# Splitting attention queries and keys where they are computed, and loading the gate weights first, in a hybrid decoder layer

## The chip, the cores and the metric

The kernel runs on one core of a Trainium2 chip. The metric is the device time of one execution in microseconds (us), the median of several. A core has a matrix engine (TensorE, PE in the profile; its weight loads are PEld), a vector engine (VectorE, DVE), an activation engine (ScalarE, ACT), a general engine (GpSimd, POOL) and a queue engine (SyncE, SP). Each runs its own instructions in program order and waits on semaphores for the others. Transfers between the device memory and the on-chip memory are DMAs, here issued by SP and by POOL, and carried out by 16 DMA engines that all queues share.

## The reference

One layer, 256 tokens, width 2048, all in fp32. `x` is normalised and multiplied by one wide projection; its columns feed two branches, which are gated, projected, merged and projected again.

```python
proj = rmsnorm(x, pre_norm_g) @ w_in
(a_q, a_k, a_v, a_g, a_lr, b_q, b_k, b_v, b_g, m_a, m_b) = split(proj)
# branch a: gated linear attention, 4 heads
gk  = log_sigmoid(a_lr @ gla_gk_w2 + gla_gk_b) / 16        # a_lr has 16 columns
o_a = rmsnorm(gla_chunked(a_q, a_k, a_v, gk), gla_norm_g) * silu(a_g)
# branch b: causal differential attention, 16 heads, two maps of width 64 each
p   = softmax(mask(q_m @ k_m.T / 8))                       # m = 0, 1
o_b = (p[0] - lam * p[1]) @ b_v
o_b = rmsnorm(o_b, diff_norm_g) * (1 - lam_init) * silu(b_g)
merged = sigmoid(m_a) * (o_a @ w_branch_a) + sigmoid(m_b) * (o_b @ w_branch_b)
out = x + rmsnorm(merged @ w_out, post_norm_g)
```

## The kernel before

**Products of parts.** Each fp32 operand is split into two parts, `hi` (a rounded copy, made by ACT) and `lo` (what is left, a DVE subtraction); a product is the sum of hi·hi, hi·lo and lo·hi. The weights come from one packed array: SP loads them as tiles `raw` of 1 MiB (128 x 2048) into three buffers, and each half of a tile is split by ACT (L263) and DVE (L264) some halves ahead of its use. A half is 8 matmuls with `hi` and 4 with `lo` (L452).

**Order of the work.** A recording layer takes the instructions as the code issues them and a scheduler orders each engine's program from a model of times; only those wrapped in `tc.keep_in_program_order` keep their place. The main line of the code is the stream of weight halves. Between halves, `pump()` advances generators ("tasks") by one turn each; a `yield` ends a turn.

1. First come the values of the linear-attention branch (`first_joint`, `token_major`), with the tasks `load_constants`, `forget_gate` and the sums of input columns.
2. The set stage computes more columns as six sets of block products with sums of weights, which POOL loads by adding DMAs (tiles `a`, `b`) and SP fills up (`c`). `others()` runs beside it and computes, among other columns, the attention queries `dq` and keys `dk` of head groups 0 and 1 (`EARLY`).
3. Then come the gates and scores of the linear attention, and after them the differential attention, group by group (`diff_heads(g)`, g = 0 to 3): the group's values `dv` and gates `ub`, for groups 2 and 3 its `dq` and `dk`, and one task `diff_pair(g, pair, values)` for each pair of heads, which runs while the columns of the next group or of the merge gates (`m02`, `m03`) and the first output products with `oah`/`oal` keep PE busy.
4. Last come the output products, the merge and the norm.

**Queries and keys.** A `dq` or `dk` tile holds a pair of heads (128 x 512 numbers, 256 KB). It is computed in fp32 by `head_part` and spilled to device memory whole by one POOL DMA (`spill`, L129). In turn 1 `diff_pair` fetches it back: `twice` (L946 to L950) writes it into both halves of the partitions, `dq` into the tile `kh` and `dk` into `kl`, four DMAs on SP. In turn 2 it makes the parts, in place: ACT rounds `kh` into `q2` (L964), DVE puts the rest into the other half of each map of `q2` (L967, twice), ACT rounds `kl` into `kh` (L968) and DVE subtracts (L969), so that `kh` and `kl` end up as the key's two parts. Then each head's scores are 8 matmuls with `kh` (L985) and `kl` (L986), DVE masks and takes maxima (L990, L991) and ACT exponentiates (L996, tiles `prob`).

**Gate weights.** `a_lr @ gla_gk_w2` needs the 16 x 1024 matrix `w2` in four copies, at partitions 0, 32, 64 and 96, in the tile `w2_raw` (`w_raw` in the trace). `load_constants` clears the tile with DVE (L336) and loads the copies with four POOL DMAs (L338) after its last mask tile. `forget_gate` takes the transposed `a_lr` (`lrt`), makes the parts of w2 (`w_s` on ACT L537, `w2h` on ACT L538, `w_s` on DVE L539) and multiplies them (L548, PE); ACT adds the bias into `gp` (L551) and goes on to the exponentials `e`. The tiles `r1h`, `s2h`, `s4h` and `r3h` that stand near it on ACT (L617) are parts of sums of the input.

Of the kernel before, what the change touches and what calls it, by code (L numbers as in the profile page):

```python
# [6 lines left out]
F32 = mybir.dt.float32  # L7
F32R = mybir.dt.float32r
BF16 = mybir.dt.bfloat16
U8 = mybir.dt.uint8  # L10
AF = mybir.ActivationFunctionType
ALU = mybir.AluOpType
AX = mybir.AxisListType

P = 128
D = 2048
S = 256
# [77 lines left out]
def hybrid_kernel(ctx: ExitStack, tc, xt, xn, preg, postg, w, w2, gkb, glag, lamv, diffg, ident_d, causal_d, lmask_d, out):  # L95
# [25 lines left out]

    def t2(shape, name):
        count[0] += 1
        return pools[0].tile(shape, F32, tag="t2", name=f"{name}_{count[0]}", bufs=5 if len(pools) == 1 else 12)

    def spill(t, name):
        count[0] += 1
        d = dram.tile(list(t.shape), t.dtype, name=f"{name}_{count[0]}")
        pool.dma_start(d, t)  # L129
        return d  # L130
# [10 lines left out]
    def f32(ap):  # L141
        return ap.bitcast(F32)
# [175 lines left out]
    diffg_s = const.tile([P, 1], F32, name="diffg_s")  # L318
    lam_s = sm([P, 4, 64], "lam_s", bufs=1)

    w2_tile = []

    def load_constants():
        tc.keep_in_program_order(sp.dma_start(ident, ident_d))
        for t, src in ((gkb_s, gkb), (glag_s, glag), (diffg_s, diffg), (causal, causal_d)):
            tc.keep_in_program_order(sp.dma_start(t, src))
        tc.keep_in_program_order(sp.dma_start(lam_s, lamv.partition_broadcast(P)))
        yield
        for n in range(0, len(LEVELS) + 2, 4):
            m = min(4, len(LEVELS) + 2 - n)  # L330
            t = u([P, 4, S], "lmask")
            tc.keep_in_program_order(sp.dma_start(t[:, :m, :], lmask_d[:, n : n + m, :]))
            pool.tensor_copy(lmask[:, n : n + m, :], t[:, :m, :])
            yield
        w2_tile.append(lend("s2h", "w2_raw"))
        tc.keep_in_program_order(dve.memset(w2_tile[0], 0.0))  # L336
        for i in range(4):
            pool.dma_start(w2_tile[0][32 * i : 32 * i + RANK, :], w2)  # L338

    ones = const.tile([P, P], F32, name="ones")  # L340
    dve.memset(ones, 1.0)
# [174 lines left out]
    def lend(tag, name, dtype=F32):  # L516

        count[0] += 1
        return blocks.tile([P, 8, P], dtype, tag=tag, name=f"{name}_{count[0]}", bufs=1).rearrange("p a t -> p (a t)")

    def forget_gate():
        w2_raw = w2_tile[0]
        yield
        bank = ps("bg")
        for b in range(2):
            pe.transpose(bank[:, P * b : P * b + P], lr[:, b, :], ident)
        top = t2([P, 512], "lrh").bitcast(F32R)
        lrt = sm([P, S], "lrt", F32R, bufs=1)
        act.activation(top[:, :S], bank[:, :S], AF.Copy)
        for i in (0, 64):  # L530
            act.activation(lrt[i : i + 32, :], bank[i : i + 32, :S], AF.Copy)
            r = slice(i + 32, i + 64)
            dve.tensor_tensor(out=lrt[r, :], in0=bank[r, :S], in1=f32(top[r, :S]), op=ALU.subtract)
        w2_s = lend("s2l", "w2_s", F32R)
        top = lend("r3h", "w2h", F32R)
        r = slice(64, P)
        act.activation(w2_s[:64, :], w2_raw[:64, :], AF.Copy)  # L537
        act.activation(top[r, :], w2_raw[r, :], AF.Copy)  # L538
        dve.tensor_tensor(out=w2_s[r, :], in0=w2_raw[r, :], in1=f32(top[r, :]), op=ALU.subtract)  # L539
        yield  # L540
        gp.extend(u([P, 2, 4, P], "gp") for _ in range(2))
        for hf in range(2):
            for c in range(2):
                bank = ps("bg")
                for i in range(2):
                    ct = 4 * hf + 2 * c + i
                    o = bank[:, S * i : S * i + S]
                    pe.matmul(o, w2_s[:, P * ct : P * ct + P], lrt, start=True, stop=True)  # L548
                for i in range(2):
                    ct = 4 * hf + 2 * c + i  # L550
                    act.activation(gp[hf][:, :, 2 * c + i, :], bank[:, S * i : S * i + S].rearrange("p (b t) -> p b t", b=2), AF.Identity, bias=gkb_s[:, ct : ct + 1])  # L551
            yield
        e = [lend(tag, "e") for tag in ("r3h", "r3l")]
        z = [t.rearrange("p b c t -> p (b c t)") for t in gp]
        for hf in range(2):
            act.activation(e[hf], z[hf], AF.Abs)
            yield
            act.activation(e[hf], e[hf], AF.Exp, scale=-1.0)
            yield
        for hf in range(2):  # L560
            act.activation(e[hf], e[hf], AF.Ln, bias=1.0)
        for hf in range(2):
            yield
            dve.scalar_tensor_tensor(out=z[hf], in0=z[hf], scalar=0.0, in1=e[hf], op0=ALU.min, op1=ALU.subtract)
        done.add("gate")
# [71 lines left out]
    def late():  # L637
        norm_row()
        yield
        lam()  # L640
        yield
# [22 lines left out]
    def head_part(t, o, o2, scaled):  # L664
        act.activation(t, o2, AF.Copy)
        dve.tensor_tensor(out=t, in0=o, in1=t, op=ALU.add)
        if scaled:
            dve.tensor_tensor(out=t, in0=t, in1=rstd_bc, op=ALU.mult)

    def others():  # L670
        banks = [ps("bg"), ps("bg")]
        for q in range(KT // 2):
            half_tile(banks, VG[4], q, x_ops, *take("v4"))
            if q == KT // 2 - 1:
                evacuate(start, banks, VG[4], 0)
            yield
        bc = rstd_bc.rearrange("p (b t) -> p b t", b=2)
        for hf in range(2):
            for name in ("k", "q"):
                part = u([P, 2, 4, P], name)  # L680
                for c in range(4):
                    o = ps("bg")
                    for h in range(2):
                        half_channel(o, h, *take(f"{name}{hf}{c}"))
                        if h:
                            o1, o2 = (t.rearrange("p (b t) -> p b t", b=2) for t in (o[:, :S], o[:, S:]))
                            t = part[:, :, c, :]
                            act.activation(t, o2, AF.Copy)
                            dve.tensor_tensor(out=t, in0=o1, in1=t, op=ALU.add)
                            if name == "k":  # L690
                                dve.tensor_tensor(out=t, in0=t, in1=bc, op=ALU.mult)
                            if c == 3:
                                ts[name, hf] = spill(part, name)
                        yield
        for g in EARLY:
            for pair in range(2):
                for name in ("dq", "dk"):
                    t = t2([P, 2, S], name)
                    for c in range(2):
                        o = ps("bg")  # L700
                        for h in range(2):
                            half_channel(o, h, *take(f"{name}{g}{2 * pair + c}"))
                            if h:
                                head_part(t[:, c, :], o[:, :S], o[:, S:], name == "dk")
                                if c:
                                    heads[g, pair, name] = spill(t, name)
                            yield
        banks = [ps("bg"), ps("bg")]
        for q in range(KT // 2):
            half_tile(banks, 512, q, x_ops, *take("m00"))  # L710
            if q == KT // 2 - 1:
                merge_gate(banks)
            yield
# [229 lines left out]

    obh, obl = [], []

    def twice(t, d):  # L946

        for h in range(2):
            rows = slice(64 * h, 64 * h + 64)
            sp.dma_start(f32(t[rows]), d.rearrange("(m p) i t -> p m i t", m=2))  # L950

    def diff_pair(g, pair, values):
# [5 lines left out]
        if not values:  # L958
            values.extend(fetch(gspill[2 * g + 4 + i], name, u, sp) for i, name in enumerate(("dv", "ub")))
        q2, kh, kl = (u([P, 2, 2, S], name, F32R) for name in ("q2", "kh", "kl"))  # L960
        twice(kh, heads[g, pair, "dq"])
        twice(kl, heads[g, pair, "dk"])
        yield
        tc.keep_in_program_order(act.activation(q2, f32(kh), AF.Copy))  # L964
        for m in range(2):
            other = slice(64 - 64 * m, P - 64 * m)
            dve.tensor_tensor(out=q2[other, m], in0=f32(kh[other, m]), in1=f32(q2[other, m]), op=ALU.subtract)  # L967
        tc.keep_in_program_order(act.activation(kh, f32(kl), AF.Copy))  # L968
        dve.tensor_tensor(out=kl, in0=f32(kl), in1=f32(kh), op=ALU.subtract)  # L969
        yield  # L970
        vv, uu = values
        heads_of = [dict(h=2 * pair + i) for i in range(2)]
# [76 lines left out]
    def diff_heads(g):  # L1049
# [15 lines left out]
        for pair in range(2):  # L1065
            for name in () if g in EARLY else ("dq", "dk"):
                t = t2([P, 2, S], name)
                for c in range(2):
                    head_part(t[:, c, :], *channel_major(f"{name}{g}{2 * pair + c}"), name == "dk")
                    pump(2)  # L1070
                heads[g, pair, name] = spill(t, name)
            tasks.append(diff_pair(g, pair, values))


# [194 lines left out]
```

## Time and profile before

| | |
|---|---|
| median of 3 runs | 1119.35 us (1118.45 to 1119.95) |
| profiled execution, first to last instruction (span) | 1121.6 us |
| instructions | 15155 |
| mean granted clock of TensorE | 0.994 |
| data moved by DMA | 266.16 MB, mean 237 GB/s |
| read from device memory / written | 244.20 MB / 20.97 MB |

The profile gives no time of its own for the profiled execution beside its span; the span is 2.25 us (0.2%) above the median of the timed runs, so sums made on the span are taken off that median.

In the rows that follow, a row of the timeline reads: start, duration, engine, line, operation, tiles written <- tiles read, shape, how many; in brackets the idle time ahead of it and what ended it. A row of a table by stretches gives the stretch and its length, then the busy time (and number of instructions) of PE, PEld, DVE, ACT and POOL, then the granted clock of TensorE (1.00 is full speed), the busy share of the DMA engines and what they moved in GB/s. A row of waits names the waiting engine and line, whom it waited for, the sum in us, how many times and the longest.

### The profile page before, as it was taken

Reading aid. Unit: us, or ns where it says so; the run is one execution under the profiler, and the core shown is the slowest. Engines: PE = TensorE matmul, PEld = TensorE weight load, DVE = VectorE, ACT = ScalarE, POOL = GpSimd, SP = SyncE. Lnnn points to the kernel's source line nnn. Section 1 sums busy time; section 2 is a strip of 40 time slices with the busy share of each in tenths; the row PEclk is TensorE's granted clock in tenths of the full one; section 3 lists DMA queues with packets and bytes.
Section 4 is the critical chain, followed back from the end, with each engine's and each line's share of the span. In section 5 each row is a group of like instructions: output and inputs, shape, how many; then the busy total and the mean of one; then the engine's idle time right before and its main releaser. Section 6 shows DMA issues by size and latency. Waiting matters only on the chain. (4 is left out here: it accounts for less than half of the span.)

```text
span 1121.6 us, 15155 instructions
## 1 busy us (share of the span) xinstructions
PE 1101.9 (98%) x5546; PEld 944.8 (84%) x5546; DVE 851.3 (76%) x1185; ACT 673.9 (60%) x975; POOL 111.2 (10%) x172
## 2 busy tenths in 40 slices
PE   8989999999999999999999999999999999999997
PEld 7989888888888888888888888888888788888886
DVE  6786987978979889799898757958676764665463
ACT  7886666666666656666555555757575643444460
POOL 0201111121021210210200000010101010000000
PEclk9999999999999999999999999999999999999999
DMA  8979959789798897974945675858568575556752
GB/s 318 301 233 317 289 219 317 178 274 302 262 312 220 302 229 230 320 221 163 337 152 179 210 256 174 271 198 270 196 198 255 196 262 201 187 184 214 271 200 75
DMA packets 54042, 266.16 MB, mean 237 GB/s; under 512 B 6672, under 2 KB 8208, under 8 KB 34512
## 3 DMA queue, kind: packets, MB, share of 16 engines
q1 hardware_dynamic: 34848, 188.11, 48.5%
q0 software_dynamic: 18112, 75.77, 24.3%
q10 hardware_dynamic: 1008, 1.32, 0.4%
q8 instruction: 43, 0.70, 0.2%
q14 instruction: 31, 0.25, 0.1%
HBM read 244.20 MB, written 20.97 MB: 236 GB/s over the span
## 5 line engine op out<-in xcount | busy, mean ns | idle before, releaser
L263 ACT ACTIVATE hi<-raw 128x1024 fp32r<-128x1024 f32 (+3 forms) x291 | 299.5, 1033 | 316.8 <-PE mm L452 212.3
L264 DVE TENSOR_TENSOR lo<-raw,hi 128x1024 fp32r<-128x1024 f32 (+3 forms) x291 | 345.3, 1189 | 179.4 <-ACT hi L263 175.8
L452 PE MATMUL mm<-hi,xs 128*128 128x512 f32 (+1 forms) x864 | 218.7, 388 | 0.2 <-ACT hi L263 0.2
L452 PEld LDWEIGHTS mm<-hi,xs 128*128 128x128 f32 x864 | 160.6, 189 | 26.9 <-ACT hi L263 0.5
L452 PE MATMUL bg<-xs,hi 128*128 128x512 f32 x512 | 131.9, 389 | 0.0
L264 DVE TENSOR_TENSOR lo<-a,hi 128x1024 fp32r<-128x1024 f32 x96 | 115.8, 1219 | 10.2 <-ACT hi L263 8.9
L452 PE MATMUL mm<-lo,xs 128*128 128x512 f32 (+1 forms) x432 | 119.6, 384 | 0.1
L263 ACT ACTIVATE hi<-a 128x1024 fp32r<-128x1024 f32 x96 | 101.7, 1060 | 26.2 <-PE mm L452 23.4
L452 PEld LDWEIGHTS bg<-xs,hi 128*128 128x128 f32 x512 | 96.3, 188 | 18.7
L452 PEld LDWEIGHTS mm<-lo,xs 128*128 128x128 f32 x432 | 81.4, 189 | 15.2 <-DVE lo L264 0.4
L452 PEld LDWEIGHTS bg<-xs,lo 128*128 128x128 f32 x512 | 69.8, 190 | 5.0
L452 PE MATMUL bg<-xs,lo 128*128 128x256 f32 x512 | 71.4, 282 | 0.0
L452 PE MATMUL mm<-xs,hi 128*128 128x512 f32 x256 | 67.3, 394 | 0.0
L264 DVE TENSOR_TENSOR lo<-b,hi 128x1024 fp32r<-128x1024 f32 x48 | 57.8, 1222 | 7.8 <-ACT hi L263 7.0
L263 ACT ACTIVATE hi<-b 128x1024 fp32r<-128x1024 f32 x48 | 50.8, 1060 | 15.4 <-PE mm L452 13.6
L452 PEld LDWEIGHTS mm<-xs,hi 128*128 128x128 f32 x256 | 46.1, 189 | 7.6
L452 PE MATMUL mm<-hi,oah 128*128 128x512 f32 x128 | 50.9, 398 | 0.0
L452 PE MATMUL mm<-hi,obh 128*128 128x512 f32 x128 | 50.4, 394 | 0.0
L452 PE MATMUL mm<-hi,oal 128*128 128x512 f32 x128 | 50.3, 393 | 0.0
L452 PE MATMUL mm<-hi,obl 128*128 128x512 f32 x128 | 49.9, 390 | 0.0
L996 ACT ACTIVATE prob<-prob,mx,score_scale 128x128 f32<-128x128 f32 x64 | 34.1, 536 | 10.9 <-DVE mx L991 10.9
L452 PE MATMUL mm<-hi,mh 128*128 128x512 f32 x96 | 37.5, 390 | 0.0
(286 smaller groups left out, 1874.6 us busy)
## 6 DMA issues: line engine op xcount, KB each, us to landing
raw<-in_w_dram SPq DMA_DIRECT2D x128, 1024.0 KB, 5.2
c<-in_w_dram SPq DMA_DIRECT2D x24, 512.0 KB, 10.2
a<-in_w_dram POOLq DMA_DIRECT2D x24, 512.0 KB, 12.1
b<-in_w_dram POOLq DMA_DIRECT2D x24, 512.0 KB, 8.4
raw<-in_w_dram SPq DMA_DIRECT2D x14, 832.0 KB, 6.9
a<-in_w_dram POOLq DMA_DIRECT2D x10, 1024.0 KB, 5.2
b<-in_w_dram POOLq DMA_DIRECT2D x10, 1024.0 KB, 7.5
kh<-dq SPq DMA_DIRECT2D x16, 256.0 KB, 8.1
```

Source lines behind the costliest of these rows:

```text
L263: act.activation(hi_t[:, a:b], r[:, a:b], AF.Copy)
L264: dve.tensor_tensor(out=lo_t[:, a:b], in0=r[:, a:b], in1=f32(hi_t[:, a:b]), op=ALU.subtract)
L452: i = pe.matmul(*args, **kw)
L996: act.activation(prob[m][:, lo:up], prob[m][:, lo:up], AF.Exp, scale=score_scale[:, b : b + 1], bias=mx[:, i : i + 1], accum_out=z[:, i : ...
```

## The change

It has three parts.

1. A query or key tile is split where it is computed (`split_spill`): ACT makes the high part `dh`, a tile of its own from a ring that grows from 5 to 6 buffers, DVE leaves the low part in place, and both are spilled, by two POOL DMAs of 256 KB instead of one.
2. `diff_pair` fetches the parts straight into the operands of the scores: `q2` by four DMAs of 64 x 512 (`place`, 128 KB each), `kh` and `kl` by two each as before. That is 8 DMAs and 1.5 MiB for a pair instead of 4 and 1 MiB. Turn 2 has no instruction left.
3. The gate weights' tile is taken at the very front, cleared by POOL, and loaded by four SP DMAs ahead of `ident`. The three instructions that split it are kept in program order.

```diff
-        return pools[0].tile(shape, F32, tag="t2", name=f"{name}_{count[0]}", bufs=5 if len(pools) == 1 else 12)
+        return pools[0].tile(shape, F32, tag="t2", name=f"{name}_{count[0]}", bufs=6 if len(pools) == 1 else 12)
...
-    w2_tile = []
+    w2_tile = [blocks.tile([P, 8, P], F32, tag="s2h", name="w2_raw", bufs=1).rearrange("p a t -> p (a t)")]
+    pool.memset(w2_tile[0], 0.0)
 
     def load_constants():
+        for i in range(4):
+            tc.keep_in_program_order(sp.dma_start(w2_tile[0][32 * i : 32 * i + RANK, :], w2))
         tc.keep_in_program_order(sp.dma_start(ident, ident_d))
...
-        w2_tile.append(lend("s2h", "w2_raw"))
-        tc.keep_in_program_order(dve.memset(w2_tile[0], 0.0))
-        for i in range(4):
-            pool.dma_start(w2_tile[0][32 * i : 32 * i + RANK, :], w2)
...
-        act.activation(w2_s[:64, :], w2_raw[:64, :], AF.Copy)
-        act.activation(top[r, :], w2_raw[r, :], AF.Copy)
-        dve.tensor_tensor(out=w2_s[r, :], in0=w2_raw[r, :], in1=f32(top[r, :]), op=ALU.subtract)
+        late = tc.keep_in_program_order
+        late(act.activation(w2_s[:64, :], w2_raw[:64, :], AF.Copy))
+        late(act.activation(top[r, :], w2_raw[r, :], AF.Copy))
+        late(dve.tensor_tensor(out=w2_s[r, :], in0=w2_raw[r, :], in1=f32(top[r, :]), op=ALU.subtract))
...
+    def split_spill(t):
+        hi = t2([P, 2, S], "dh")
+        act.activation(hi.bitcast(F32R), t, AF.Copy)
+        dve.tensor_tensor(out=t, in0=t, in1=hi, op=ALU.subtract)
+        return spill(hi, "dh"), spill(t, "dl")
...
-                                    heads[g, pair, name] = spill(t, name)
+                                    heads[g, pair, name] = split_spill(t)
...
+    def place(t, d, m, h):
+        sp.dma_start(f32(t[64 * h : 64 * h + 64, m]), d[64 * m : 64 * m + 64])
...
-        twice(kh, heads[g, pair, "dq"])
-        twice(kl, heads[g, pair, "dk"])
-        yield
-        tc.keep_in_program_order(act.activation(q2, f32(kh), AF.Copy))
         for m in range(2):
-            other = slice(64 - 64 * m, P - 64 * m)
-            dve.tensor_tensor(out=q2[other, m], in0=f32(kh[other, m]), in1=f32(q2[other, m]), op=ALU.subtract)
-        tc.keep_in_program_order(act.activation(kh, f32(kl), AF.Copy))
-        dve.tensor_tensor(out=kl, in0=f32(kl), in1=f32(kh), op=ALU.subtract)
+            for h in range(2):
+                place(q2, heads[g, pair, "dq"][h != m], m, h)
+        for t, d in zip((kh, kl), heads[g, pair, "dk"]):
+            twice(t, d)
+        yield
         yield
...
-                heads[g, pair, name] = spill(t, name)
+                heads[g, pair, name] = split_spill(t)
```

The scheduler places the instructions anew. Three places follow. First ACT around the forget gate, about 56 to 67 us into the run before; a number behind a name tells buffers apart. Before:

```order
ACTIVATE lrt_604<-bg_600 32x256
ACTIVATE w_s_610<-w_raw_514 64x1024
ACTIVATE hi_681<-raw_615 128x832
ACTIVATE r1h<-temp_765 128x1024
ACTIVATE w2h_611<-w_raw_514 64x1024
ACTIVATE hi_704<-raw_679 128x832
ACTIVATE hi_727<-raw_679 128x832
ACTIVATE s2h<-temp_765 128x1024
ACTIVATE gp_633<-bg_635,gkb_s 128x2x128 x2
```

And now:

```order
ACTIVATE lrt_604<-bg_600 32x256
ACTIVATE w_s_610<-w_raw 64x1024
ACTIVATE w2h_611<-w_raw 64x1024
ACTIVATE hi_681<-raw_615 128x832
ACTIVATE gp_633<-bg_635,gkb_s 128x2x128 x2
ACTIVATE gp_633<-bg_640,gkb_s 128x2x128 x2
ACTIVATE gp_634<-bg_661,gkb_s 128x2x128 x2
ACTIVATE gp_634<-bg_666,gkb_s 128x2x128 x2
ACTIVATE e_697<-gp_633 128x1024
ACTIVATE hi_704<-raw_679 128x832
```

The two halves of the split now follow `lrt` and each other; `r1h` and `s2h` have gone out of this stretch, behind the `hi` of later half tiles (`r1h` behind that of the half that PE starts at 79.40 in the run before), and `hi_704` stands behind the eight `gp`. PE's matmuls L548 moved up by one half tile, into the `lo` matmuls of the half before.

The second place is SP at group 3, about 848 to 861 us into the run before, from one `raw` tile on. Before:

```order
DMA raw_727_7820<-in_w_dram 128x2048
DMA dv_719_7803<-gl_317_4749 128x1024
DMA ub_720_7805<-gr_310_4662 128x1024
DMA kh_722_7808<-dq_579_6814 64x2x512 x2
DMA kl_723_7809<-dk_607_6998 64x2x512 x2
DMA raw_731_7866<-in_w_dram 128x2048
DMA kh_729_7860<-dq_631_7158 64x2x512 x2
DMA kl_730_7861<-dk_648_7293 64x2x512 x2
DMA raw_738_7928<-in_w_dram 128x2048
```

And now:

```order
DMA kh_753_7882<-dh_633_7062 64x2x512 x2
DMA kl_754_7883<-dl_634_7064 64x2x512 x2
DMA q2_759_7932<-dh_659_7227 64x512
DMA q2_759_7932<-dl_660_7229 64x512 x2
DMA q2_759_7932<-dh_659_7227 64x512
DMA kh_760_7933<-dh_678_7371 64x2x512 x2
DMA kl_761_7934<-dl_679_7373 64x2x512 x2
DMA raw_762_7943<-in_w_dram 128x2048
DMA raw_769_8000<-in_w_dram 128x2048
```

Ahead of these stand, as before, the same `raw` tile, `dv`, `ub`, and the four DMAs of the first pair's `q2`. The tile that was `raw_731` and is now `raw_762` stood between the fetches of the two pairs, and now follows both. In groups 0 to 2 the fetches of a pair stand where they stood or up to three `raw` tiles earlier.

The third place is ACT at the same point, about 867 to 877 us into the run before; `hi_382` and `hi_383` are the halves of that tile. Before:

```order
ACTIVATE hi_381_7868<-raw_727_7820 128x1024
ACTIVATE kh_722_7808<-kl_723_7809 128x1024
ACTIVATE hi_382_7884<-raw_731_7866 128x1024
ACTIVATE prob0_732_7900,z_735_7903<-prob0_732_7900,mx_734_7902,score_scale_120 128x128
ACTIVATE prob0_732_7900,z_735_7903<-prob0_732_7900,mx_734_7902,score_scale_120 128x256
ACTIVATE prob1_733_7901,z_735_7903<-prob1_733_7901,mx_734_7902,score_scale_120 128x128
ACTIVATE prob1_733_7901,z_735_7903<-prob1_733_7901,mx_734_7902,score_scale_120 128x256
ACTIVATE q2_728_7859<-kh_729_7860 128x1024
ACTIVATE hi_383_7930<-raw_731_7866 128x1024
ACTIVATE kh_729_7860<-kl_730_7861 128x1024
```

And now:

```order
ACTIVATE hi_381_7945<-raw_758_7898 128x1024
ACTIVATE prob0_763_7977,z_766_7980<-prob0_763_7977,mx_765_7979,score_scale_122 128x128
ACTIVATE prob0_763_7977,z_766_7980<-prob0_763_7977,mx_765_7979,score_scale_122 128x256
ACTIVATE prob1_764_7978,z_766_7980<-prob1_764_7978,mx_765_7979,score_scale_122 128x128
ACTIVATE prob1_764_7978,z_766_7980<-prob1_764_7978,mx_765_7979,score_scale_122 128x256
ACTIVATE prob0_771_8039,z_774_8042<-prob0_771_8039,mx_773_8041,score_scale_122 128x128
ACTIVATE prob0_771_8039,z_774_8042<-prob0_771_8039,mx_773_8041,score_scale_122 128x256
ACTIVATE prob1_772_8040,z_774_8042<-prob1_772_8040,mx_773_8041,score_scale_122 128x128
ACTIVATE hi_382_7961<-raw_762_7943 128x1024
ACTIVATE hi_383_8002<-raw_762_7943 128x1024
```

The splits of `q2` and `kh` are gone, and `hi_382`, which stood ahead of the first head's exponentials, now stands behind these and three of the second head's. On PE the scores of the second and the third head stand back to back ahead of the matmuls with `hi_382`.

## The prediction before the result was known

> **What bounds the kernel now.** I read the page's busy times first, then TensorE's waits.
>
> ```profile
> PE 1101.9 (98%) x5546; PEld 944.8 (84%) x5546; DVE 851.3 (76%) x1185; ACT 673.9 (60%) x975; POOL 111.2 (10%) x172
> ```
> ```profile
> PE bg L985 <- ACT kh L968: 4.2, 4, 2.5
> PE bg L548 <- DVE w_s L539: 2.9, 1, 2.9
> ...
> PE bg L986 <- DVE kl L969: 1.0, 4, 0.3
> ```
>
> PE is busy in 98% of the span, and the change leaves every matmul in place. It can only win what PE loses by waiting, or add waits. The second list (who waits, for whom: sum, times, longest) names the waits that the change touches: 2.9 us for w_s, the gate weights' split, and 4.2 + 1.0 us in front of the attention scores for kh and kl, the key's two parts. What a wait costs beyond its idle time is read from the granted clock, here around the wait for w_s (stretch, its length, then busy times; PEclk third from the right):
>
> ```profile
> 65.00:67.00 2.00, 2.00 (x12) 1.97 (x13) 2.00 (x3) 1.97 (x5) 0.00 (x0) 0.79 0.53 220
> 67.00:70.00 3.00, 3.00 (x12) 2.87 (x11) 3.00 (x4) 3.00 (x8) 0.00 (x0) 0.57 0.50 131
> ```
>
> After the gap PE works at 0.79 and then at 0.57: 2 × 0.21 + 3 × 0.43 = 1.7 us more lost. The Trainium skill ("TensorE: Matmul & The Clock Gate", section "Why this matters for your kernels") says that only idle gaps over about 3 us bring the clock down. By it a 2.86 us gap costs no clock time, and the sum below would come to −5.3 us instead of −7.0, so 1114.1; the row says otherwise, and the row decides.
>
> **Part 1: the gate weights.** The chain that ends in the wait:
>
> ```profile
> 55.82 0.38 ACT L531 ACTIVATE lrt<-bg 32x256 fp32r<-32x256 f32 x1
> 59.48 1.06 ACT L537 ACTIVATE w_s<-w_raw 64x1024 fp32r<-64x1024 f32 x1 [3.28 <-DMA w_raw<-in_w_dram]
> 60.45 0.88 ACT L263 ACTIVATE hi<-raw 128x832 fp32r<-128x832 f32 x1
> 61.23 1.04 ACT L617 ACTIVATE r1h<-temp 128x1024 fp32r<-128x1024 f32 x1
> 62.30 1.05 ACT L538 ACTIVATE w2h<-w_raw 64x1024 fp32r<-64x1024 f32 x1
> 63.62 1.22 DVE L539 TENSOR_TENSOR w_s<-w_raw,w2h 64x1024 fp32r<-64x1024 f32 x1
> ```
> ```profile
> 59.14 0.92 PE L452 MATMUL mm<-lo,xs 128*128 128x416 f32 x4
> 64.99 1.15 PE L548 MATMUL bg<-lrt,w_s 128*128 128x256 f32 x8 [2.86 <-DVE w_s L539]
> 79.40 1.78 PE L452 MATMUL mm<-hi,xs 128*128 128x416 f32 x8 [0.19 <-ACT hi L263]
> ```
>
> ACT sits 3.28 us until the weights land, and hi and r1h stand between its two halves of the split. With the load among the first constants, w_raw is there long before 56; w_s, w2h and DVE's subtraction then follow lrt directly. ACT starts at 55.82 + 0.38 = 56.20; w_s takes 0.97 to the next start, w2h 1.05, DVE 1.22: ready at 59.4. L548 moves up into the lo matmuls that began at 59.14, at about 59.6, so its wait goes, and the slow clock with it: 2.86 + 1.71 = 4.57.
>
> What is late next is ACT, which has no gap from 59.48 to the hi of the half tile that PE starts at 79.40:
>
> ```profile
> 78.38 2.54 ACT L263 ACTIVATE hi<-raw 128x832 fp32r<-128x832 f32 x3
> ```
>
> The first of these three (0.85) ends at 79.23: 19.75 us of ACT work. After, it starts at 56.20; r1h and s2h (2.1) have moved behind this hi; and ACT waits about 0.95 for L548's first result (its hi after the split ends at 59.0, L548's first result comes at 60.0). That gives 56.20 + 19.75 − 2.1 + 0.95 = 74.8, against PE's own arrival at 79.40 − 0.19 − 4.57 = 74.6. A wait of 0.2 stays: **−4.4**. If ACT kept r1h and s2h ahead this would fall to −2.3; with no wait at all it is −4.6. Four more issues on SP in front of ident push the constants and weight tiles behind them back by some 2 us; the list above has no wait of PE for them, so I cost this at 0, at worst 2. The memset moves to POOL, which has nothing else at the front.
>
> **Part 2: the small waits of groups 0 to 2.** Waits of PE from 640 to 870, and one stretch of group 0 that holds some of them:
>
> ```profile
> PE bg L985 <- ACT kh L968: 1.8, 3, 0.6
> PE bg L986 <- DVE kl L969: 1.0, 4, 0.3
> 700.00:716.00 16.00, 15.08 (x94) 12.80 (x92) 14.22 (x30) 11.23 (x19) 0.54 (x1) 1.00 0.96 308
> ```
>
> They sum to 2.8, of which 0.2 belongs to group 3. PE idles 0.92 of those 16 us, in three gaps, and the clock stays 1.00, so they are worth their idle time. The splits that cause them go from the scores' path:
>
> ```profile
> L968 ACT ACTIVATE kh<-kl 128x1024 fp32r<-128x1024 f32 x8 | 8.5, 1060 | 4.4 <-ACT hi L263 2.8 <-ACT dk L665 1.2 <-DMA kl<-dk 0.4
> L964 ACT ACTIVATE q<-kh 128x1024 fp32r<-128x1024 f32 x8 | 8.4, 1046 | 0.0
> L967 DVE TENSOR_TENSOR q<-kh,q 64x512 fp32r<-64x512 f32 x16 | 11.0, 687 | 0.5
> L504 ACT ACTIVATE obh<-bg,diffg_s 128x512 fp32r<-128x512 f32 x8 | 5.5, 686 | 1.4 <-PE bg L1043 1.4
> 357.31 0.69 DVE L767 TENSOR_TENSOR gr<-mm,p 128x512 f32<-128x512 f32 x1
> ```
>
> A pair loses 2.1 us of ACT and about 2.6 of DVE (2 × 0.69, and 1.2 for kl, a subtraction of the size of w_s's), and gains two copies and two subtractions of 512 columns, which cost at most 2 × 0.69 on each engine by the last two rows, where nothing waits for them but the spill. kh, kl and q2 then come straight from the DMA. In groups 0 to 2 their fetches are issued as early as before or up to three weight tiles earlier, so I take the wait as gone: **−2.6**, and 0 as its other end (a transfer late by as much as the split was).
>
> **Part 3: group 3.** The longest wait, 2.47 us:
>
> ```profile
> 873.35 0.22 PE L985 MATMUL bg<-kh,q 128*128 128x128 f32 x1
> 874.27 0.40 PE L452 MATMUL mm<-hi,oah 128*128 128x512 f32 x1
> 877.37 0.44 PE L985 MATMUL bg<-kh,q 128*128 128x128 f32 x2 [2.47 <-ACT kh L968]
> 878.00:880.00 2.00, 2.00 (x10) 1.69 (x9) 2.00 (x3) 0.27 (x1) 0.00 (x0) 0.64 0.84 221
> 880.00:881.00 1.00, 1.00 (x5) 0.90 (x5) 1.00 (x10) 0.00 (x0) 0.00 (x0) 0.50 1.06 434
> 881.00:884.00 3.00, 3.00 (x13) 2.46 (x12) 2.25 (x9) 2.95 (x8) 0.00 (x0) 0.84 0.15 63
> ```
>
> It goes, with its slow clock of 2 × 0.36 + 0.5 + 3 × 0.16 = 1.7, and so does 0.2 ahead of the head before. But here the order changes for the worse. SP issues all fetches of both pairs ahead of the next weight tile, and ACT's hi of that tile (hi_382) now stands behind three exponentials of the head whose scores begin at 873.35:
>
> ```profile
> 869.84 0.28 DVE L990 CUSTOM_DVE_ANT_0 prob<-bg,causal 128x128 f32<-128x128 f32 x1
> 871.26 0.49 ACT L996 ACTIVATE prob<-prob,mx,score_scale 128x128 f32<-128x128 f32 x1 [2.60 <-DVE mx L991]
> 872.82 0.59 ACT L996 ACTIVATE prob<-prob,mx,score_scale 128x256 f32<-128x256 f32 x1
> 867.60 1.06 ACT L263 ACTIVATE hi<-raw 128x1024 fp32r<-128x1024 f32 x1 [1.95 <-DMA raw<-in_w_dram]
> ```
>
> Those scores take 0.92 (873.35 to 874.27). DVE's maxima, 1.4 us in the rows (869.84 to 871.26), run partly beside them and end near 875.3 with one maximum of the next head in between; three exponentials take 1.56 (871.26 to 872.82); hi 1.06: 877.9. PE, after the next head's scores, needs it at 874.27 + 0.92 = 875.2. It waits 2.7, about the old 2.47 + 0.2, and long enough for the same slow clock.
>
> The transfer decides nothing as long as that tile lands by 876.9:
>
> ```profile
> DMA packets 2306, 8.41 MB, mean 263 GB/s; under 512 B 256, under 2 KB 256, under 8 KB 1792
> ```
>
> From that stretch (846 to 878): before, 5.24 MB stand up to that tile's end (by their shapes 1 MiB for the tile ahead of it, which SP issues at 847.8, 1 for dv and ub, 1 for a pair, 1 for two loads of POOL, 1 for the tile itself), by 263 GB/s 19.9 us from 847.8, so 867.7; hi started at 867.60. After, 2.1 MB more stand ahead: 7.34 MB, 27.9 us, 875.7. It just makes it. Part 3 is **0**; its ends are −4.4 (both waits gone) and, at the 212 GB/s that full DMA engines (0.91) move in the row 340 to 360 below, a landing at 882.4, its hi at 883.5 and so +5.6.
>
> **The set stage** pays for half of the new splits. DVE has no room at three places there:
>
> ```profile
> 340.00:360.00 20.00, 20.00 (x105) 17.16 (x104) 19.92 (x22) 12.30 (x14) 3.08 (x4) 1.00 0.91 212
> 420.00:440.00 20.00, 20.00 (x103) 17.05 (x102) 19.98 (x22) 13.73 (x15) 1.02 (x2) 1.00 0.71 200
> 480.00:500.00 20.00, 20.00 (x97) 16.85 (x96) 19.99 (x22) 12.52 (x14) 5.06 (x7) 1.00 0.71 163
> 363.53 0.62 PE L452 MATMUL mm<-lo,xs 128*128 128x512 f32 x2
> 361.93 1.22 DVE L264 TENSOR_TENSOR lo<-c,hi 128x1024 fp32r<-128x1024 f32 x1
> ```
>
> PE's busy time is full in all three, so the lo tiles still arrive in time; the thinnest cover is 363.53 − 363.15 = 0.4 us. Four of the eight new subtractions fall into such stretches. I cost them at 0, at worst 0.69 each. Eight more spills (2 MB) share POOL's queue with the sets' weight loads; DMA's share there is 0.7 to 0.9, so I take 0 too.
>
> **Sum:** −4.4 − 2.6 + 0 = −7.0 on a profiled span of 1121.6, 2.25 us above the median 1119.35 that I subtract from: **1112.4**. Differences under 0.2% (2.2 us) count as none.
>
> **Rivals.**
> - *Group 3's wait goes altogether* (hi_382 early enough): −11.4, 1108.0. Against it stands the order on ACT. 0.08.
> - *Only one part works*: fetches arrive as late as the splits did (−4.4, 1115.0), or the weights land late all the same and only part 2 gains (−2.6, 1116.8). The 0.96 DMA share at 700 to 716 speaks for the first, the free front for neither. 0.15.
> - *The tile at group 3 lands late*: from 876.9 on 1 us for each us, up to +5.6, 1118.0. For it: the transfers ahead of it are 2.1 MB more, and the margin is 1.2 us. Against it: the mean of that stretch. 0.15.
> - *Slower: the set stage's DVE.* Each subtraction in a full stretch makes a lo late, and PE cools each time as at 65 to 70: 4 × (0.7 + 1.7) = +9.6, with the sum 1122.0. It decides once the stretches' cover, 0.4 to 1 us, is used up by several subtractions together and the gaps reach some 2.5 us; gaps of 0.6 left the clock at 1.00. 0.07.
> - *None of it shows*: the gains of part 1 are eaten by ACT and part 2's by DMA. 0.05.
>
> My forecast has 0.5. The range 1107.8 to 1117.8 holds it, the first three rivals and parts of the unknown costs, and leaves out the last two. Faster 0.87, same 0.06, slower 0.07.
>
> **What would show it.** Right: no wait of L548 on w_s and a clock of 1.00 from 65 to 70 less the shift; the half at 79.40 about 4.4 earlier; no waits in front of scores in groups 0 to 2; in group 3 one wait of PE for ACT hi of 2 to 3 us followed by a low clock. Wrong: hi of that tile ended by a DMA instead of the exponentials; waits for lo between 340 and 520; a wait of w_s that stays.

## The result and the profile after

The changed kernel took 1113.55 us (median of 4, 1112.5 to 1114.47), the kernel before 1118.9 us in the same comparison: ratio 0.9949, 95% interval 0.9932 to 0.9965, so 5.7 us less (3.9 to 7.6). A second comparison, in the experiments below, gave 0.9929 (0.9916 to 0.9941). The forecast was 1112.4 us, 7.0 less than before.

The waits of PE after:

```profile
PE mm L451 <- ACT hi L263: 3.4, 2, 3.0
PE bg L345 <- DVE ones_b L342: 1.6, 1, 1.6
PE bg L439 <- ACT hi L263: 0.7, 1, 0.7
```

The wait for `w_s` and all waits in front of the scores are gone. In their place stands one of 3.05 us for ACT's `hi`, and a small one of 0.33.

Where the time went is read from the start of the same matmul in both traces, row by row (timeline, PE). Before:

```profile
11.49 0.95 PE L440 MATMUL bg<-hi,xs 128*128 128x416 f32 x4
639.48 0.72 PE L864 MATMUL bg<-xq,xk 128*128 128x128 f32 x5
825.19 1.09 PE L452 MATMUL mm<-hi,xs 128*128 128x512 f32 x4
882.71 0.39 PE L452 MATMUL mm<-hi,oah 128*128 128x512 f32 x1
```

After:

```profile
9.92 0.92 PE L439 MATMUL bg<-hi,xs 128*128 128x416 f32 x4
633.73 0.49 PE L870 MATMUL bg<-xq,xk 128*128 128x128 f32 x3
814.69 1.07 PE L451 MATMUL mm<-hi,xs 128*128 128x512 f32 x4
873.60 0.40 PE L451 MATMUL mm<-hi,oah 128*128 128x512 f32 x1
```

| stretch of the run before | shift at its end | gained in it | forecast |
|---|---|---|---|
| to 12 us (start) | −1.57 | 1.6 | 0 |
| 12 to 639 (gate weights; set stage) | −5.75 | 4.2 | 4.4 |
| 639 to 825 (groups 0 to 2) | −10.50 | 4.75 | 2.6 |
| 825 to 883 (group 3) | −9.11 | −1.4 | 0 |

From 883 on both run alike; the spans are 1121.6 and 1112.5. The 9.1 us between them are probably more than the change is worth, since the traced execution of before is a long one: of 41 timed executions of that kernel in the comparisons below one has a span above 1121.6, and their medians are 1118.6 to 1119.9. The times above decide.

The first row of the table cannot be put down to the change from these two traces. Before had the clock at 0.72 in its start, after at 1.00, and the experiment with group 3's `hi` first, whose code at the front is that of the changed kernel, had 0.72 again. The rows from 6 to 12, in this order:

```profile
6.00:12.00 6.00, 4.60 (x17) 4.23 (x16) 4.25 (x8) 4.93 (x10) 0.00 (x0) 0.72 1.04 418
```
```profile
6.00:12.00 6.00, 5.34 (x27) 4.84 (x26) 4.32 (x8) 4.98 (x10) 0.00 (x0) 1.00 1.03 417
```
```profile
6.00:12.00 6.00, 3.55 (x11) 3.42 (x12) 3.36 (x6) 4.04 (x8) 0.00 (x0) 0.72 1.02 407
```

In all the traces of this document, the matmul that starts at 13.03 us in the run before starts at 13.0 to 13.2 in the three with the old front and at 11.1 to 14.7 in the ten with the new one, seven of these below 12. Whether the new front has a share in this stays open; the first experiment speaks against the full 1.6 us. So the start alone can move a span by some 3 us, and spans are compared stretch by stretch.

At the gate weights, after:

```profile
54.62 1.07 ACT L537 ACTIVATE w_s<-w_raw 64x1024 fp32r<-64x1024 f32 x1
55.72 1.06 ACT L538 ACTIVATE w2h<-w_raw 64x1024 fp32r<-64x1024 f32 x1
58.18 1.18 PE L548 MATMUL bg<-lrt,w_s 128*128 128x256 f32 x8
73.67 1.77 PE L451 MATMUL mm<-hi,xs 128*128 128x416 f32 x8 [0.33 <-ACT hi L263]
```

The split follows `lrt`, L548 has no wait, and the half that PE started at 79.40 now starts at 73.67: 5.73 earlier, of which 1.57 are the start's. ACT is what comes late next: 0.33 us, where 0.2 was forecast.

At group 3, after:

```profile
862.41 0.22 PE L991 MATMUL bg<-kh,q 128*128 128x128 f32 x1
864.81 0.49 ACT L1002 ACTIVATE prob<-prob,mx,score_scale 128x128 f32<-128x128 f32 x1 [4.24 <-DVE mx L997]
867.46 0.79 PE L451 MATMUL mm<-hi,oah 128*128 128x512 f32 x1 [3.05 <-ACT hi L263]
865.89 0.48 ACT L1002 ACTIVATE prob<-prob,mx,score_scale 128x128 f32<-128x128 f32 x1
866.37 1.04 ACT L263 ACTIVATE hi<-raw 128x1024 fp32r<-128x1024 f32 x1
866.00:868.00 2.00, 0.54 (x1) 0.50 (x2) 0.72 (x2) 2.00 (x4) 0.00 (x0) 0.69 0.87 360
868.00:870.00 2.00, 2.00 (x6) 1.56 (x5) 1.96 (x4) 2.00 (x6) 0.00 (x0) 0.50 0.05 20
870.00:872.00 2.00, 2.00 (x6) 1.52 (x6) 1.97 (x4) 2.00 (x8) 0.00 (x0) 0.50 0.55 123
872.00:874.00 2.00, 2.00 (x7) 1.56 (x6) 1.93 (x6) 0.96 (x2) 0.00 (x0) 0.60 0.95 401
```

`hi` starts the moment the third exponential lets it. The gap is followed by 0.50, 0.50 and 0.60: 1.0 + 1.0 + 0.8 = 2.8 us of lost clock from 868 on. PE works again from 867.46, and the clock is at 0.50 there too, which adds 0.3: 3.1 us, against 1.7 behind the old gap.

### The profile page after: what moved, and what is told of

The parts are those of the page before. It is cut to its first block, busy times and chain, and to the rows that moved or that the text cites. A ratio compares the mean times of both kernels' runs of the same rounds, so it can differ in the third digit from the quotient of the medians.

```text
span 1112.5 us, 15209 instructions
## 1 busy us (share of the span) xinstructions
PE 1098.4 (99%) x5546; PEld 943.9 (85%) x5546; DVE 839.3 (75%) x1176; ACT 666.9 (60%) x975; POOL 120.7 (11%) x185
## 4 chain that ended last, share of the span: by engine, by line
PE 97%; ACT 1%; DVE 1%; issue 1%; DMA 0%; DVEq 0%; SPq 0%; POOLq 0%; POOL 0%; ACTq 0%
PE mm L451 66%; PE bg L451 19%; PE bg L439 2%; PE mm L424 2%; PE mm L439 2%; PE bg L870 1%; PE bg L424 1%; PE bg L992 1%; PE bg L991 1%; DMA raw<-in_w_dram 0%; PE bg L1016 0%; PE bg L1027 0%; PE bg L1028 0%; PE bg L1026 0%; PE bg L1124 0%
```

## The experiments

All ratios are against the kernel before, run on the same chip beside it, with 95% intervals. My theory was that the three places above each have the cause that the prediction named, with two terms mis-sized.

**The gate weights alone.** The changed kernel with the queries' and keys' part undone:

```diff
-                heads[g, pair, name] = split_spill(t)
+                heads[g, pair, name] = spill(t, name)
...
+        twice(kh, heads[g, pair, "dq"])
+        twice(kl, heads[g, pair, "dk"])
+        yield
...
```

> Before with the gate weights' part alone (load at the front, the three split instructions kept in order); queries and keys as before. My theory: this part is worth 4.3 us (the half tile at 79.40 starts that much earlier once the start of the run is set aside), so 1118.9 - 4.3 = 1114.6 us. Rival: the 1.6 us by which the changed kernel is ahead already at 12 us belongs to the new order at the front, so this part is worth 5.9 us: 1113.0 us, and its trace is 1.6 us ahead of the one of before at 12 us. The waits in front of the scores stay as before, 5.2 us in all.

Measured: 1117.7 us, ratio 0.9975 (0.9965 to 0.9985), 2.8 us less (1.7 to 3.9). In its trace the half at 79.40 is 4.1 ahead once the 1.5 of its start are taken off, close to the 4.3 expected; but the wait at group 3 is 3.45 instead of 2.47, so 1.1 is given back there:

```profile
863.12 1.06 ACT L263 ACTIVATE hi<-raw 128x1024 fp32r<-128x1024 f32 x1 [2.94 <-DMA raw<-in_w_dram]
872.88 0.44 PE L994 MATMUL bg<-kh,q 128*128 128x128 f32 x2 [3.45 <-ACT kh L977]
```

The first row shows why: ACT waits 2.94 for the weight tile, where it waited 1.95, and everything behind it on ACT, the splits of `q2` and `kh` too, shifts. The rival (5.9 us, the start included) is out: even less the 1.1 it would be 4.8, above the interval. Between 83 and 866 its trace keeps the same distance to before, so nothing else in those 780 us cares for the earlier arrival.

**The queries and keys alone.** The kernel before with parts 1 and 2 of the change.

> Before with the queries' and keys' part alone; gate weights as before. My theory: groups 0 to 2 gain 4.6 us (a wait costs PE more than the idle time that the profile shows, since the last matmul's shown end lies some 0.17 us behind the point from which PE could go on), group 3 loses 1.8 us by a longer wait with a longer slow clock: 1118.9 - 2.8 = 1116.1 us; the wait for w_s stays at 2.9 us. Rival, as in my prediction: the waits are worth their idle time alone, 2.6, so 1118.9 - 2.6 + 1.8 = 1118.1 us.

Measured: 1117.37 us, ratio 0.9972 (0.9962 to 0.9983), 3.1 less (1.9 to 4.3). The rival's 0.8 is out. My 2.8 holds as a number, but not as a sum: in the trace groups 0 to 2 gain 4.8 us, and group 3 loses 0.2 where I expected 1.8. The two parts measured apart give 5.9 us, the whole 5.7 and 8.0.

Its wait for `w_s` was 3.3 us, and 1.3 in another run with the old front (parts 1 and 2 with the second pair held back, below). The four POOL DMAs took 7.8 to 8.4 us to land in the first and 5.6 to 7.0 in the second; in the run before it was 7.3 to 8.3, for a wait of 2.9. In the run with the short wait PE then waits 1.7 us for the `hi` of the half at 79.40, and the clock stays at 1.00. So what the gate weights' part is worth depends on the run that it is taken against: up to 83 us, with the start taken off, the changed kernel gains 4.1 us on before, 4.6 on this run and 2.6 on the other.

**What makes the wait at group 3: the order on ACT, or the tile?** First the second pair's fetches held back, which moves both:

```diff
+        if (g, pair) == (3, 1):
+            yield
+            yield
         q2, kh, kl = (u([P, 2, 2, S], name, F32R) for name in ("q2", "kh", "kl"))
```

> The changed kernel, with the second pair's task of group 3 held back by two turns, so that its fetches stand behind two weight tiles on SP and ACT's hi of the tile after the first pair stands ahead of the exponentials. My theory: the wait of 3.05 us and the slow clock behind it (2.9 us) both go: 1113.5 - 5.9 = 1107.6 us, clock 1.00 at 866 to 874. Rival: the fetches that are issued later arrive late for the third head's scores, and a wait of 2 to 3 us stands there instead: 1111 to 1114 us.

Measured: 1109.25 us, ratio 0.9894 (0.988 to 0.9909). Waits of PE, and the stretch in question:

```profile
PE bg L345 <- DVE ones_b L342: 1.6, 1, 1.6
PE mm L451 <- ACT hi L263: 0.3, 1, 0.3
```
```profile
866.00:872.00 6.00, 6.00 (x29) 4.97 (x28) 3.71 (x9) 4.62 (x12) 0.00 (x0) 1.00 1.04 360
```

The wait and the slow clock are gone, and no new wait stands in front of the scores: against the changed kernel 0.9949 − 0.9894, or 0.9929 − 0.9894, is 6.2 or 3.9 us; 5.9 was expected. This version beats both kernels.

Then the order alone, with the transfers left as they are:

```diff
+            if 380 <= j < 385:
+                tc.keep_in_program_order(i)      # i: ACT's hi of half j
...
+                    if (g, pair) == (3, 0):
+                        tc.keep_in_program_order(e)   # e: ACT's exponential
```

> The changed kernel with the transfers as they are, but the hi instructions of the halves 380 to 384 and the exponentials of group 3's first pair kept in program order, so that hi of the disputed half stands ahead of the exponentials on ACT. My theory: the exponentials set the 3.05 us; the tile lands 0.7 us after PE arrives, hi takes 1.06, so a wait of about 1.8 us stays, with some of the slow clock: 1109.5 to 1112.3 us. Rival: the transfer sets the wait, it stays at 3 us or more, 1113.5 us or above.

Measured: 1112.55 us, ratio 0.9923 (0.9907 to 0.9938). By its ratio it lies between the two, as expected, but the interval also holds the changed kernel's second ratio, so the trace has to decide:

```profile
867.62 1.06 ACT L263 ACTIVATE hi<-raw 128x1024 fp32r<-128x1024 f32 x1 [11.65 <-DMA raw<-in_w_dram]
868.74 0.80 PE L453 MATMUL mm<-hi,oah 128*128 128x512 f32 x1 [2.01 <-ACT hi L263]
```

`hi` now waits for its tile and nothing else, and PE still waits 2.0. So the exponentials set the end of the 3.05 us, but behind them the tile would have set 2.0: only 1.0 hung on the order, and both had to move. The margin between the two, 1.2 us in my prediction, comes out as 1.0.

**The slow clock: the gap, or the moment?** The changed kernel, this time measured again beside it, with the gap filled by matmuls that nobody reads:

```diff
+                if (g, pair) == (3, 1) and part is scores and w is one:
+                    idle = ps("bg")
+                    for _ in range(24):
+                        tc.keep_in_program_order(pe.matmul(idle[:, :S], q2[:, 0, 0, :P], kh[:, 0, 0, :], start=True, stop=True))
```

> The changed kernel itself, as the measure for the runs beside it. If the two parts add up as they measured apart (ratios 0.9975 and 0.9972), the ratio is 0.9947; the waits are 3.0 us for the hi at group 3 and none in front of the scores.

> The changed kernel with 24 more matmuls of 256 columns on PE, whose result nobody reads, right behind the third head's scores of group 3 and ahead of the half that waits; every other instruction keeps its place. They take about 2.8 us, the length of the gap. My theory: the gap and not the moment brings the clock down; hi comes when it came, PE starts the half when it did, the clock stays 1.00 and 2.9 us of slow clock are saved: 2.9 us under the changed kernel, ratio 0.992. Rival: the slow clock has another cause (the transfers and exponentials that run then), nothing is saved: the time of the changed kernel, ratio 0.9947, or up to 2.8 us more where the added matmuls delay the half.

Measured: 1113.12 us, 0.9929 (0.9916 to 0.9941), for the changed kernel, so that the 0.9947 of the two parts lies just outside; 1112.86, 0.9922 (0.9908 to 0.9935), with the filled gap. The traces, first of the filled gap, then of the changed kernel measured again:

```profile
865.68 3.04 PE L1048 MATMUL bg<-kh,q 128*128 128x256 f32 x24
868.89 0.50 PE L451 MATMUL mm<-hi,oah 128*128 128x512 f32 x1 [0.18 <-ACT hi L263]
870.00:872.00 2.00, 2.00 (x11) 1.64 (x10) 1.93 (x6) 2.00 (x6) 0.00 (x0) 1.00 0.03 12
```
```profile
868.00:870.00 2.00, 2.00 (x8) 1.63 (x7) 1.96 (x4) 2.00 (x6) 0.00 (x0) 0.71 0.06 25
870.00:872.00 2.00, 2.00 (x6) 1.52 (x6) 1.97 (x5) 2.00 (x8) 0.00 (x0) 0.50 0.56 131
872.00:874.00 2.00, 2.00 (x10) 1.61 (x9) 1.93 (x5) 1.01 (x2) 0.00 (x0) 0.93 0.93 393
```

With PE kept at work the clock stays at 1.00 at the same moment, with the same transfers and the same `hi`: the gap makes the slow clock. Of the 2.9 us that I expected the times show 0.8, with intervals of 1.4 to either side, so they don't settle the size. The traces do for themselves: from 866 to 883 of the run before, the filled gap gains 1.6 us on the changed kernel measured again and 2.8 on its first trace.

So the same gap of 3.05 us had two prices: 0.6 + 1.0 + 0.1 = 1.7 us in the second trace, 3.1 in the first. Read as time at 0.50, the rows give 3.4 us in the second trace, and as much behind both old gaps in the run before, but 6.8 in the first trace of the changed kernel. In all traces of this document together ten gaps of 2.0 to 3.45 us behind the first 20 us of the run were each followed by such a stretch; nine of the stretches took 3.4 us, so 1.7 us is the common price, and the first trace of the changed kernel is the exception. What made its stretch twice as long is not shown. The timed runs fit two prices: of nine executions of the changed kernel the four with a mean clock of 0.995 took 1113.58 to 1114.47 us, the five with 0.996 or 0.997 1112.5 to 1113.12.

**Is it the load or the order that helps at the gate weights?** The first experiment without the three `keep_in_program_order`:

> Before with the gate weights loaded at the front, without keeping their three split instructions in program order; queries and keys as before. The split then stands ahead of lrt, and the matmuls L548 two half tiles earlier on PE, ahead of the point where lrt is ready. My theory: the wait for w_s goes, but PE waits about 2 us for lrt, so that about half of the gain is left: ratio 0.998 to 0.999, against 0.9975 with the order kept. Rival: the load alone is what counts, ratio 0.9975 or less.

Measured: 1116.9 us, ratio 0.9962 (0.9948 to 0.9977). My theory fell: L548 has no wait for `lrt`, since I had placed it a half tile too early in time.

```profile
36.66 1.04 ACT L536 ACTIVATE w_s<-w_raw 64x1024 fp32r<-64x1024 f32 x1
40.13 1.06 ACT L537 ACTIVATE w2h<-w_raw 64x1024 fp32r<-64x1024 f32 x1
53.89 0.38 ACT L530 ACTIVATE lrt<-bg 32x256 fp32r<-32x256 f32 x1
54.88 1.18 PE L547 MATMUL bg<-lrt,w_s 128*128 128x256 f32 x8
72.70 1.68 PE L451 MATMUL mm<-hi,xs 128*128 128x416 f32 x8
PE bg L993 <- ACT kh L976: 4.2, 4, 2.5
```

The load alone is enough. Free of its fixed place the split runs at 36 to 41 us, ahead of the stretch where ACT is full, and the half that waits 0.33 in the changed kernel waits for nothing. Its times lie below those of the first experiment, with intervals that overlap. The wait at group 3 is 2.5 here, as in the run before (last row), and not the 3.45 of the first experiment: the 1.1 us given back there belong to that one run, and not to an earlier arrival as such.

**Room on DVE in the set stage.** The changed kernel with one more DVE instruction in each split:

```diff
         dve.tensor_tensor(out=t, in0=t, in1=hi, op=ALU.subtract)
+        dve.tensor_tensor(out=t, in0=t, in1=t, op=ALU.max)
```

> The changed kernel with one more DVE instruction of 512 columns (a maximum of the low part with itself, which changes nothing) in each of the 16 splits. It asks how near the set stage's DVE is to its limit. My theory: the thinnest cover of a lo there is 0.5 us in the changed kernel, one instruction takes 0.65, so single waits of 0.1 to 0.8 us appear between 340 and 520, 0.5 to 3 us in all, without a slow clock: up to 3 us above the changed kernel. Rival: DVE still has room, the time of the changed kernel. Second rival, from my prediction: each late lo cools PE, 6 us and more above it.

Measured: 1114.23 us, ratio 0.9934 (0.9918 to 0.995), the changed kernel's time. PE is busy without a gap from 340 to 520, at full clock, with DVE at 166 of 180 us:

```profile
340.00:520.00 180.00, 180.00 (x892) 152.81 (x891) 165.88 (x173) 121.24 (x136) 32.29 (x48) 1.00 0.84 257
```

My theory of single waits fell here too, and with it the prediction's slower rival: even twice the added DVE work finds room, in an order that the scheduler has made anew.

**What the waits in front of the scores cost in all.** Parts 1 and 2 alone with the second pair of group 3 held back:

> Before with the queries' and keys' part alone, and group 3's second pair two turns later; gate weights as before. It asks what the waits in front of the scores cost in all. My theory: the waits of groups 0 to 2 cost 4.6 us, more than their idle time of 2.6, and group 3's 4.4 (0.2 + 2.5 idle, 1.7 slow clock): 9 us under before, ratio 0.992. Rival: idle time and slow clock alone, 2.6 + 4.4 = 7.0 us, ratio 0.9938.

Measured: 1113.3 us, ratio 0.9924 (0.9912 to 0.9937): 8.5 us less (7.1 to 9.9). My 9.0 holds; the rival's 7.0 (0.9938) lies just outside. In the trace groups 0 to 2 gain 4.8 us and group 3 gains 4.6; another 1.5 us come from this run's shorter wait for `w_s`, which is not the edit's.

**Both findings together.**

> The changed kernel with group 3's second pair two turns later, again, as the measure for the run beside it: ratio 0.9894.

> The changed kernel with both findings: group 3's second pair two turns later, and the gate weights' split not kept in program order. Theory: the two add up, as they stand 800 us apart; against the second pair's delay alone (ratio 0.9894) another 0.5 to 1.4 us: ratio 0.988 to 0.989. Rival: the second finding was noise of the start of the run, ratio 0.9894 or above.

Measured: 1108.25 us, 0.9886 (0.9868 to 0.9904), and 1106.89 us, 0.9869 (0.9856 to 0.9883). The second is the fastest version; its only waits on PE beyond the start are 0.2 us. That it beats the first by 1.9 us lies within the two intervals. In the traces it is 0.9 us ahead of the first between 12 and 83 us, where the free split works.

## Why the prediction held, and where its steps were off

The total was right: 7.0 us forecast, 5.7 and 8.0 measured. Luck had a part in it: part 2 was worth 2.1 us more than forecast, and in the first trace of the changed kernel group 3 gave 1.4 back. In its second trace, of the comparison that measured 8.0, group 3 gave back 0.2, close to the 0 forecast, and nothing else made up for part 2: without the start that trace gains 8.7 us.

*Part 1, −4.4:* the trace shows 4.2 in that stretch, no wait of L548, a clock of 1.00, and ACT as the next one late by 0.33. The chain of the prediction held step by step. What it left out is that the wait it starts from is not the same in every run (1.3 to 3.3 us in three traces). Neither of the other ends that it named, −2.3 and −4.6, came about in the changed kernel.

*Part 2, −2.6:* the mechanism was right and the size was off: 4.75. The step that failed is "so they are worth their idle time". The profile counts a matmul as busy until its modelled end, which lies about 0.17 us behind the next one's start (0.39 long, one every 0.23 us). A wait that begins there shows that much less, and one shorter than that shows nothing. In group 0 before, and the same matmuls without a wait after:

```profile
711.66 2.00 PE L452 MATMUL mm<-xs,hi 128*128 128x512 f32 x8
714.25 0.44 PE L985 MATMUL bg<-kh,q 128*128 128x128 f32 x2 [0.59 <-ACT kh L968]
714.53 1.16 PE L452 MATMUL mm<-xs,lo 128*128 128x256 f32 x8
715.72 0.44 PE L986 MATMUL bg<-kl,q 128*128 128x128 f32 x2
```
```profile
698.86 2.00 PE L451 MATMUL mm<-xs,hi 128*128 128x512 f32 x8
700.70 1.11 PE L451 MATMUL mm<-xs,lo 128*128 128x256 f32 x8
701.66 1.78 PE L451 MATMUL mm<-xs,hi 128*128 128x512 f32 x7
```

After, the eight matmuls with `hi` take 1.84 us from start to start, those with `lo` 0.96. Before, 711.66 + 1.84 = 713.50, so L985 at 714.25 is 0.75 late, not 0.59; and 714.53 + 0.96 = 715.49, so L986 at 715.72 is 0.23 late where no wait is shown at all. All waits of groups 0 to 2 can be read like this. In the traces the usual distance to the next matmul's start is 0.23 us behind a matmul of 512 columns, 0.12 behind one of 256 and 0.11 behind one of 128. Against these, eight matmuls of the scores are late in the run before by 0.18 to 0.76 us, 3.9 in all, where the profile shows 2.6 of idle time; in the changed kernel none is late by over 0.1. So 1.3 of the missing 2.1 us are the modelled ends, eight times 0.16. The rest, some 0.9, lies in delays of under 0.1 us each, and what causes them is not shown. The whole comes out the same in every trace without the splits (4.75 to 4.8), and the timed 8.5 agrees.

*Part 3, 0:* the place and the cause were right, behind the exponentials, the landing of the tile close behind them as well. The length was 3.05 where 2.7 was forecast: the exponentials begin 2.4 us after the start of the second head's scores (862.41 to 864.81), where the sum has 1.95 (873.35 to 875.3). The clock, 1.7 us taken from behind the old gap, held in the second trace, where the stretch lost 0.2 in all. In the first trace it was 3.1, and with the 0.4 gained ahead of it the stretch lost 1.4 us. The filled gap shows that the clock follows the gap.

*The set stage, 0*, held: no wait for a `lo`, and room for as much again. The slower rival is refuted; the rival in which the tile lands late did not come about, but the tile was only 1.0 us from deciding. The range was said to hold that rival; its end, 1118.0, lies 0.2 above it.

The Trainium skill ("TensorE: Matmul & The Clock Gate", section "Why this matters for your kernels") warns of idle gaps over about 3 us. In these traces shorter ones were enough: the old gaps of 2.47 and 2.86 us brought the clock down, and the one of 2.0 us with the `hi` ahead did so too, with 0.56 behind it. The gaps of 1.3 and 1.7 us in the run with parts 1 and 2 and the second pair held back left it at 1.00. The row behind the gap of 2.0 us:

```profile
870.00:872.00 2.00, 2.00 (x6) 1.58 (x6) 1.10 (x6) 2.00 (x6) 0.00 (x0) 0.56 0.11 45
```

## What to carry to other kernels

Taking an operation off the path is half of the edit; the other half is what the scheduler and the queues do with the room. Here moving the fetches closer together put a weight tile behind 2 MiB more and its split behind three exponentials, and gave back in one wait what the removed waits at that place had cost; holding one task back by two turns won it back, and the third experiment is faster than the change. When waits on a full engine are summed, take the distance from start to start against a stretch without a wait, not the idle time shown. Add the slow clock behind each gap that is as long as those that brought it down in the traces, here 2 us or more, as a range: 1.7 us in nine cases of ten, 3.1 in one. Before a size is read from one trace, see whether its span is a usual one for that kernel.

## What the runs showed of the hardware that was not expected

The slow clock behind a gap came in stretches of one length: 3.4 us at 0.50 behind nine of ten gaps of 2.0 to 3.45 us, whatever the gap's length, and twice that behind one. Behind one and the same gap of 3.05 us at group 3 it cost 1.7 us in one run and 3.1 in another. At the start of the run, the ten traces with the new front reached the same matmul at 11.1 to 14.7 us. These differences are of the size of the change's terms, and are the reason why single profiles of this kernel are compared by stretches.
